# Latents expanded one token tile behind their projection, both roots in one computation, three landing buffers

## The chip, the cores and the metric

The kernel runs on one core of one Trainium2 chip. The time is device microseconds of one execution of the whole program. A core has these engines, each with its own instruction stream, which it works off in order: TensorE (PE) for matrix products and transposes, VectorE (DVE) and ScalarE (ACT) for elementwise work, GpSimd (POOL) for elementwise work too, and SyncE (SP), which issues most loads and stores. ScalarE issues loads as well (those of the feed-forward weights). Engines wait for each other by semaphores.

## The reference

A trunk of two layers over 512 latent tokens and 256 context tokens, width 1024, all in float32. Each layer: a modulated RMS norm, one input projection whose columns are split over four mixers (latent attention, retention, neighbourhood attention, windowed attention), an output projection, a gated residual, then a SwiGLU block. In the last layer the context tokens only give keys and values. The part that the change touches is the latent attention (MLA):

```python
def qkv(cq, ckv, kr, rotate):                     # cq: 256 columns, ckv: 128, kr: 32
    q  = heads(rms_norm(cq,  q_norm)  @ w_uq,  H)  # 256 -> 4 x 96
    kv = heads(rms_norm(ckv, kv_norm) @ w_ukv, H)  # 128 -> 4 x (64 + 64)
    ...
# rms_norm(x, g) = x * rsqrt(mean(x * x) + EPS) * g
```

So each token has two latents, a query and a key/value one; each is normalised by the reciprocal root of its own mean square and expanded by a matrix. Retention, which the kernel computes beside it, goes through chunks of 128 tokens in both directions: scores times a decay mask, plus queries times a state that is updated from chunk to chunk.

## The kernel before

Tokens are worked on in six tiles of 128: 0 to 3 are latent tokens, 4 and 5 context. Layer 0 takes them in the order 4, 5, 0, 1, 2, 3, layer 1 in the order 0 to 5. Every float32 product is computed as three products of rounded halves, high x high, high x low, low x high (L467 to L469), added in PSUM. A weight unit (512 KB as a rule) is loaded into a landing buffer "raw", copied to its high half "wh" by ScalarE (L449), and the rest is put in "wl" by a subtraction (L213), two times in three on VectorE and the third time on GpSimd. There are four landing buffers, five wh and seven wl; a landing buffer is free again when its wl is done.

A program-side list scheduler puts the instructions of each engine in order before anything runs: it goes by readiness and priority, so that code written in one place is spread out and mixed with others. The order that comes out is fixed; a buffer's reuse, a store ahead of it in SyncE's queue, or an instruction ahead of it on its engine can then make an instruction wait.

Around the change a layer goes like this. The retention projection (L1206 to L1228) writes queries, keys and values out and computes chunk states; L1246 updates the running states on VectorE, each a 64 x 64 multiply and add. Then comes the latent stage: `mla_proj` (L961) is a generator that does one token tile per step, and between its steps the caller starts retention chunks (`ret_chunk`, L1250). One step of the generator:

- 24 matmuls of 416 columns (the projection) into PSUM "pg", for which there are five buffers;
- ScalarE copies 384 columns to "cn", in one of two buffers named "nat" (L1052), which retention and the key split use too; two squares with a running sum give the two mean squares (L1056, L1057);
- for each latent, VectorE adds EPS (L1061) and computes the reciprocal root by `rsqrt1` (L287 to L291, eight instructions on one column, results scaled by RS1, which is divided out of w_uq and w_ukv in L966 and L973 by GpSimd);
- TensorE transposes cn (L1067), ScalarE copies the high half "cth" (L1071), VectorE subtracts to the low half "ctl" (L1072);
- six matmuls expand to queries and three to keys and values, "po"; scaled copies with the roots follow (L1080 to L1096), the key part through `k_split` (L686) and transposes (L693).

A retention chunk loads its rows (ldr, L1252), transposes, multiplies by query decays on GpSimd ("rt", L1262), forms scores (L1267), masks them on VectorE ("P", L1270) and multiplies with values (L1282) and states (L1278). At the end `merge_ret` (L1308) loads finished rows into one of two buffers "og". Here is one root as it was:

```python
def rsqrt1(a, nm):
    y = S("rs_y" + nm, 1); u = S("rs_t" + nm, 1)
    ...
    for c in (-3.0, -12.0, -768.0):
        dve.scalar_tensor_tensor(u, y, a, y, op0=ALU.mult, op1=ALU.mult)
        dve.scalar_tensor_tensor(y, u, c, y, op0=ALU.add, op1=ALU.mult)
```

Of the kernel before, what the change touches and what calls it, by code (L numbers as in the profile page):

```python
# [11 lines left out]
ALU = mybir.AluOpType  # L12
# [4 lines left out]
P = 128  # L17
# [6 lines left out]
EPS = 1e-6  # L24
RS1 = -8192.0
# [49 lines left out]

CHANGED = {'pad': {'raw': 1024}, 'bufs': {'raw': 4}}


def merged(opts):
# [6 lines left out]
def build(tc, I, out, opts=None):  # L88
# [36 lines left out]
    def T(tag, shape, dt=F32, bufs=None):  # L125
        uid[0] += 1
        if not PADB:
            return sb.tile(list(shape), dt, tag=tag, name=f"{tag}_{uid[0]}", bufs=bufs or BUFS[tag])
        st = site(tag)
        n = int(np.prod(shape[1:]))  # L130
        x = sb.tile([P, PADB[tag]], dt, tag=st, name=f"{tag}_{uid[0]}", bufs=SPB.get(st, BUFS[tag]))[0:shape[0], 0:n]
        if len(shape) == 2:
            return x
        names = "abcd"[:len(shape) - 1]
        return x.rearrange("p (%s) -> p %s" % (" ".join(names), " ".join(names)), **dict(zip(names, shape[1:])))

    def S(tag, n, bufs=3):
        uid[0] += 1
        return sb.tile([P, n], F32, tag=tag, name=f"{tag}_{uid[0]}", bufs=bufs)
# [104 lines left out]
    def vec(name, k0=0, n=1):  # L244
        i, r = VROW[name]
        return vecs[i][:, r + k0:r + k0 + n]
# [281 lines left out]
    def nat_block(w, c0, n, hT, order, rng=None, filler=None, nf=0, nxt=None):  # L528


        W = ahead.pop(c0, None) or load_nat(w, c0, n)
        for i, t in enumerate(order):
            if nxt and i == PF.get(nxt[0], 9):
                ahead[nxt[0]] = load_nat(w, *nxt)
            a, b = rng(t) if rng else (0, n)
            if a is None:
                continue
            ps = PS("g")
            for k in range(8):
                mm3(ps[:, a:b], hs(hT, t, k), (W[k][0][:, a:b], W[k][1][:, a:b]), k == 0, k == 7)  # L540
                if nf and k % (8 // nf) == 8 // nf - 1:
                    next(filler, None)
            yield t, ps
# [267 lines left out]
    for l in range(LAYERS):  # L811
# [4 lines left out]
        hT = hn  # L816
# [144 lines left out]
        def mla_proj(R):  # L961
# [1 line left out]
            raw = T("raw", [P, 2, 384])  # L963
            sp.dma_start(raw, I["mla_w_uq"][l].rearrange("(k p) n -> p k n", p=P))
            for i in range(2):
                pool.tensor_scalar(raw[:, i], raw[:, i], vec("qn%d" % l, i), 1.0 / RS1, op0=ALU.mult, op1=ALU.mult)  # L966
            wuqh = T(WU, [P, 2, 384], F32R)
            wuql = T(WU, [P, 2, 384], F32R)
            act.activation(wuqh, raw, AF.Copy)
            sub_lo(wuql, raw, wuqh)  # L970
            raw = T("raw", [P, 512])
            sp.dma_start(raw, I["mla_w_ukv"][l])
            pool.tensor_scalar(raw, raw, vec("kn%d" % l), 1.0 / RS1, op0=ALU.mult, op1=ALU.mult)  # L973
            wukv = (T("gate", [P, 512], F32R), T("gate", [P, 512], F32R))
            act.activation(wukv[0], raw, AF.Copy)
            sub_lo(wukv[1], raw, wukv[0])
# [67 lines left out]
                act.activation(d, pt[0:DR, 0:n * P], AF.Copy)  # L1044
                dve.tensor_tensor(d[32:64], pt[32:64, 0:n * P], d[32:64].bitcast(F32), op=ALU.subtract)

            for t, ps in nat_block(w_in, 0, 416, hT, order, (lambda t: (0, 416) if (t < 4 or not last) else (160, 416))):
                qn = t < 4 or not last
                a0 = 0 if qn else 256
                ss = S("ssm", 2)  # L1050
                cn = T("nat", [P, 384])
                act.activation(cn[:, a0:384], ps[:, a0:384], AF.Copy)  # L1052
                KRE.tensor_copy(R[:, t, :], ps[:, 384:416])
                sq = T(SQT, [P, 384])
                if qn:
                    act.activation(sq[:, 0:256], cn[:, 0:256], AF.Square, scale=1.0 / 16.0, accum_out=ss[:, 0:1])  # L1056
                act.activation(sq[:, 256:384], cn[:, 256:384], AF.Square, scale=float(128 ** -0.5), accum_out=ss[:, 1:2])  # L1057
                r = [None, None]
                for c in ((1, 0) if qn else (1,)):
                    ms = S("msm%d" % c, 1)  # L1060
                    dve.tensor_scalar(ms, ss[:, c:c + 1], EPS, None, op0=ALU.add)  # L1061
                    r[c] = rsqrt1(ms, "mk"[c])
                rq, rk = r
                pt = PS(M0)
                k0 = 0 if qn else 2
                for i in range(k0, 3):
# [30 lines left out]
                k_stack(kTm, kn, H, t, M3)  # L1097
                if t in (3, 5):
                    k_rope(t)
                yield mla_attn  # L1100

        def swa_proj():
# [435 lines left out]
```

## Time and profile before

| What | Value |
|---|---|
| Median of 3 runs | 1908.55 us (1906.93 to 1913.02) |
| The profiled execution itself | 1910.68 us |
| Its span, first to last instruction | 1908.8 us |
| TensorE busy | 1811.7 us, 95% |
| VectorE busy | 1187.5 us, 62% |
| ScalarE, GpSimd busy | 672.9 and 605.2 us |
| Mean granted TensorE clock | 0.985 of full speed |

How to read it: the span is that of the profiled execution, some 2 us shorter than what the device measures for it. Busy times of the engines lie beside each other, so they don't add up; an engine's idle time matters only where another one waits for it at the end of a chain. The granted clock of TensorE has two levels, 2.4 GHz (1.00) and 1.2 GHz (0.50); a stretch in between has some of each.

### The profile page before, as it was taken

How to read it: one execution, taken by the hardware profiler on the slowest of the kernel's cores; microseconds unless marked ns; L12 is line 12 of the kernel's file. 1: busy time of each engine (PE TensorE's matmuls, PEld its weight loads, DVE VectorE, ACT ScalarE, POOL GpSimd, SP SyncE). 2: the span in 40 equal slices, each digit the busy share in tenths (PEclk: the TensorE clock that was granted, in tenths of full speed). 3: DMA queues.
4: the chain of work that ended last, by engine and by line, in shares of the span. 5: the costliest groups of instructions: out<-in, count | busy, mean ns of one | idle time of the engine just before them, and what ended most of it. 6: DMA issues, size and time to landing. Idle time of an engine off the chain costs nothing. (4 is left out here: it accounts for less than half of the span.)

```text
span 1908.8 us, 28192 instructions
## 1 busy us (share of the span) xinstructions
PE 1811.7 (95%) x10447; PEld 1494.0 (78%) x10447; DVE 1187.5 (62%) x2676; ACT 672.9 (35%) x1517; POOL 605.2 (32%) x560
## 2 busy tenths in 40 slices
PE   6899999889999999999999999899889999999997
PEld 3677777778889887888888878788777888888885
DVE  5696886877898757564434293465588863434335
ACT  3325643254542221221122233564255532222223
POOL 0211113323115443444344111211333144645542
PEclk9999999899999999999999999999999999999999
DMA  7675436445124346342222222422443033232321
GB/s 226 210 206 162 131 98 187 127 151 117 50 95 127 122 155 199 105 134 63 74 67 67 57 84 91 120 75 81 143 142 100 15 115 101 84 107 89 102 86 44
DMA packets 193555, 215.22 MB, mean 113 GB/s; under 512 B 66660, under 2 KB 141578, under 8 KB 193418
## 3 DMA queue, kind: packets, MB, share of 16 engines
q10 hardware_dynamic: 75840, 111.17, 18.8%
q1 hardware_dynamic: 117578, 102.25, 18.1%
q8 instruction: 82, 1.34, 0.3%
q14 instruction: 55, 0.45, 0.1%
HBM read 192.76 MB, written 20.63 MB: 112 GB/s over the span
## 5 line engine op out<-in xcount | busy, mean ns | idle before, releaser
L469 PE MATMUL pg<-wh,b 128*128 128x512 f32 (+2 forms) x1128 | 439.9, 394 | 7.2 <-POOL b L213 6.2
L467 PE MATMUL pg<-wh,b 128*128 128x512 f32 (+2 forms) x1128 | 443.1, 393 | 1.8 <-ACT b L515 0.9
L468 PE MATMUL pg<-wl,b 128*128 128x512 f32 (+2 forms) x1128 | 441.5, 391 | 2.2 <-DVE rs_yn L288 1.8
L467 PE MATMUL ps<-b,wh 128*128 128x512 f32 (+1 forms) x1120 | 388.2, 347 | 0.0
L469 PE MATMUL ps<-b,wl 128*128 128x512 f32 (+1 forms) x1120 | 386.7, 345 | 0.8 <-DVE wl L213 0.8
L468 PE MATMUL ps<-b,wh 128*128 128x512 f32 (+1 forms) x1120 | 386.9, 345 | 0.5 <-POOL b L213 0.5
L213 DVE TENSOR_TENSOR wl<-raw,wh 128x1024 fp32r<-128x1024 f32 (+1 forms) x131 | 207.4, 1592 | 174.9 <-ACT wh L449 145.3
L449 ACT ACTIVATE wh<-raw 128x1024 fp32r<-128x1024 f32 (+1 forms) x196 | 203.8, 1049 | 271.1 <-PE pg L469 172.3
L213 POOL TENSOR_TENSOR wl<-raw,wh 128x1024 fp32r<-128x1024 f32 (+1 forms) x65 | 160.0, 2462 | 336.7 <-ACT wh L449 286.8
L1362 POOL TENSOR_TENSOR b<-b,nat 128x512 f32<-128x512 f32 (+1 forms) x204 | 217.8, 1087 | 124.0 <-DVE nat L1360 95.0
L469 PEld LDWEIGHTS pg<-wh,b 128*128 128x128 f32 x1128 | 214.9, 191 | 49.6 <-POOL b L213 9.6
L467 PEld LDWEIGHTS pg<-wh,b 128*128 128x128 f32 x1128 | 215.5, 191 | 40.9 <-ACT b L1476 1.9
L468 PEld LDWEIGHTS pg<-wl,b 128*128 128x128 f32 x1128 | 215.2, 191 | 39.7 <-DVE rs_yn L288 2.3
L467 PEld LDWEIGHTS ps<-b,wh 128*128 128x128 f32 x1120 | 213.5, 191 | 27.4 <-issue 2.4
L469 PEld LDWEIGHTS ps<-b,wl 128*128 128x128 f32 x1120 | 213.4, 191 | 26.0 <-DVE wl L213 1.0
L468 PEld LDWEIGHTS ps<-b,wh 128*128 128x128 f32 x1120 | 213.6, 191 | 25.5 <-POOL b L213 0.7
L1360 DVE TENSOR_TENSOR nat<-pg,gate 128x512 f32<-128x512 f32 x240 | 161.9, 688 | 102.0 <-PE pg L469 97.8
L1473 ACT ACTIVATE P<-ps 128x512 f32<-128x512 f32 (+1 forms) x70 | 35.4, 505 | 224.3 <-PE ps L469 128.0
L1475 DVE TENSOR_TENSOR P<-ps,P 128x512 f32<-128x512 f32 (+1 forms) x70 | 40.1, 575 | 118.9 <-PE ps L469 118.8
L1476 ACT ACTIVATE b<-P 128x512 fp32r<-128x512 f32 (+1 forms) x70 | 37.6, 538 | 195.3 <-DVE P L1475 176.0
L397 DVE SCALAR_TENSOR_TENSOR PT<-qT,consts,PT 128x512 f32<-128x512 f32 x112 | 94.0, 857 | 14.6 <-DMA qT<-in_ada_w_dram 13.3
L213 POOL TENSOR_TENSOR b<-P,b 128x512 fp32r<-128x512 f32 (+1 forms) x24 | 27.8, 1158 | 231.9 <-ACT b L1476 231.9
(322 smaller groups left out, 2441.7 us busy)
## 6 DMA issues: line engine op xcount, KB each, us to landing
raw<-in_ffn_w_dram ACTq DMA_DIRECT2D x132, 512.0 KB
qT<-in_ada_w_dram ACTq DMA_DIRECT2D x96, 256.0 KB
raw<-in_w_in_dram SPq DMA_DIRECT2D x40, 512.0 KB
a<-in_ada_w_dram SPq DMA_DIRECT2D x32, 256.0 KB
a<-in_ada_w_dram ACTq DMA_DIRECT2D x32, 256.0 KB
xn<-in_ada_w_dram ACTq DMA_DIRECT2D x32, 256.0 KB
raw<-in_w_out_dram SPq DMA_DIRECT2D x16, 512.0 KB
ldq<-q_d SPq DMA_DIRECT2D x40, 128.0 KB
```

The source lines that it names most:

```text
L213: eng.tensor_tensor(out, full, hi.bitcast(F32), op=ALU.subtract)
L397: dve.scalar_tensor_tensor(acc[s], w, sS[:, k, s:s + 1], acc[s], op0=ALU.mult, op1=ALU.add)
L449: act.activation(hi, raw_ap, AF.Copy)
L467: pe.matmul(ps, a[0], b[0], start=first, stop=False)
L468: pe.matmul(ps, a[0], b[1], start=False, stop=False)
L469: pe.matmul(ps, a[1], b[0], start=False, stop=last)
L1360: dve.tensor_tensor(tm, ps, gates[(0 if t < 4 else 2) + b], op=ALU.mult)
L1362: eng.tensor_tensor(ap, ap, tm[:, a:c], op=ALU.add)
L1473: act.activation(s1[j][:, sl], ps, AF.Silu)
L1475: dve.tensor_tensor(s1[j][:, sl], ps, s1[j][:, sl], op=ALU.mult)
L1476: act.activation(gh[j][:, sl], s1[j][:, sl], AF.Copy)
```

## The change

The number of landing buffers "raw" goes from 4 to 3. One step of the generator is split in two functions: `latent` (copy of cn, mean squares, roots) and `expand` (transposes and all that follows). A tile is expanded after the latents of the next one have been taken; the last is expanded right behind its own. cn lies in an "og" buffer instead of a "nat" one. Both mean squares of a tile go through one `rsqrt` of two columns (one column for the context tiles of layer 1), and the scale RS1 is gone from the two weights.

```diff
--- before.py
+++ after.py
@@ -75,7 +75,7 @@
 
 
 
-CHANGED = {'pad': {'raw': 1024}, 'bufs': {'raw': 4}}
+CHANGED = {'pad': {'raw': 1024}, 'bufs': {'raw': 3}}
 
 
 def merged(opts):
@@ -963,14 +963,14 @@
             raw = T("raw", [P, 2, 384])
             sp.dma_start(raw, I["mla_w_uq"][l].rearrange("(k p) n -> p k n", p=P))
             for i in range(2):
-                pool.tensor_scalar(raw[:, i], raw[:, i], vec("qn%d" % l, i), 1.0 / RS1, op0=ALU.mult, op1=ALU.mult)
+                pool.tensor_scalar(raw[:, i], raw[:, i], vec("qn%d" % l, i), 1.0, op0=ALU.mult, op1=ALU.mult)
             wuqh = T(WU, [P, 2, 384], F32R)
             wuql = T(WU, [P, 2, 384], F32R)
             act.activation(wuqh, raw, AF.Copy)
             sub_lo(wuql, raw, wuqh)
             raw = T("raw", [P, 512])
             sp.dma_start(raw, I["mla_w_ukv"][l])
-            pool.tensor_scalar(raw, raw, vec("kn%d" % l), 1.0 / RS1, op0=ALU.mult, op1=ALU.mult)
+            pool.tensor_scalar(raw, raw, vec("kn%d" % l), 1.0, op0=ALU.mult, op1=ALU.mult)
             wukv = (T("gate", [P, 512], F32R), T("gate", [P, 512], F32R))
             act.activation(wukv[0], raw, AF.Copy)
             sub_lo(wukv[1], raw, wukv[0])
@@ -1044,23 +1044,26 @@
                 act.activation(d, pt[0:DR, 0:n * P], AF.Copy)
                 dve.tensor_tensor(d[32:64], pt[32:64, 0:n * P], d[32:64].bitcast(F32), op=ALU.subtract)
 
-            for t, ps in nat_block(w_in, 0, 416, hT, order, (lambda t: (0, 416) if (t < 4 or not last) else (160, 416))):
+            def latent(t, ps):
+
                 qn = t < 4 or not last
                 a0 = 0 if qn else 256
                 ss = S("ssm", 2)
-                cn = T("nat", [P, 384])
+                cn = T("og", [P, 384])
                 act.activation(cn[:, a0:384], ps[:, a0:384], AF.Copy)
                 KRE.tensor_copy(R[:, t, :], ps[:, 384:416])
                 sq = T(SQT, [P, 384])
                 if qn:
                     act.activation(sq[:, 0:256], cn[:, 0:256], AF.Square, scale=1.0 / 16.0, accum_out=ss[:, 0:1])
                 act.activation(sq[:, 256:384], cn[:, 256:384], AF.Square, scale=float(128 ** -0.5), accum_out=ss[:, 1:2])
-                r = [None, None]
-                for c in ((1, 0) if qn else (1,)):
-                    ms = S("msm%d" % c, 1)
-                    dve.tensor_scalar(ms, ss[:, c:c + 1], EPS, None, op0=ALU.add)
-                    r[c] = rsqrt1(ms, "mk"[c])
-                rq, rk = r
+                n = 2 if qn else 1
+                ms = S("msm", 2)
+                dve.tensor_scalar(ms[:, 0:n], ss[:, 2 - n:2], EPS, None, op0=ALU.add)
+                r = rsqrt(ms[:, 0:n], n, "m%d" % n)
+                return cn, qn, r[:, 0:1], r[:, n - 1:n]
+
+            def expand(t, cn, qn, rq, rk):
+
                 pt = PS(M0)
                 k0 = 0 if qn else 2
                 for i in range(k0, 3):
@@ -1097,6 +1100,14 @@
                 k_stack(kTm, kn, H, t, M3)
                 if t in (3, 5):
                     k_rope(t)
+
+            behind = []
+            for t, ps in nat_block(w_in, 0, 416, hT, order, (lambda t: (0, 416) if (t < 4 or not last) else (160, 416))):
+                behind.append((t,) + latent(t, ps))
+                if len(behind) > 1:
+                    expand(*behind.pop(0))
+                if t == order[-1]:
+                    expand(*behind.pop(0))
                 yield mla_attn
 
         def swa_proj():
```

`rsqrt`, which was there before for retention's eight columns:

```python
def rsqrt(a, n, nm):
    y = S("rs_y" + nm, n); u = S("rs_t" + nm, n)
    dve.tensor_scalar(y.bitcast(I32), a.bitcast(I32), 1, None, op0=ALU.logical_shift_right)
    dve.tensor_scalar(y.bitcast(I32), y.bitcast(I32), -1, 0x5F3759DF, op0=ALU.mult, op1=ALU.add)
    for _ in range(3):
        dve.tensor_tensor(u, y, y, op=ALU.mult)
        dve.scalar_tensor_tensor(u, u, -0.5, a, op0=ALU.mult, op1=ALU.mult)
        dve.scalar_tensor_tensor(y, u, 1.5, y, op0=ALU.add, op1=ALU.mult)
```

Because of the scheduler the change moves instructions in many places. Three of them, in the order of the program; a row has a line, an operation, its output and inputs (tile names with their numbers) and the size. In the kernel after, lines from L1044 on are shifted (L1246 becomes L1257, L1270 becomes L1281, L1067 becomes L1070, L1072 becomes L1075).

SyncE, second w_in block of layer 0, before:

```order
L419 DMA nat_1054<-in_ada_b_dram 2x2x128 x4
L459 DMA raw_1071<-in_w_in_dram 128x2x512
L459 DMA raw_1077<-in_w_in_dram 128x2x512
L424 DMA mod_d_67<-nat_1053 2x2x128 x4
L459 DMA raw_1083<-in_w_in_dram 128x2x512
L898 DMA r_d_122<-nat_1065 128x256
L459 DMA raw_1089<-in_w_in_dram 128x2x512
L904 DMA qn_d_121<-nat_1065 128x256
```

and after:

```order
L419 DMA nat_1054<-in_ada_b_dram 2x2x128 x4
L459 DMA raw_1071<-in_w_in_dram 128x2x512
L459 DMA raw_1077<-in_w_in_dram 128x2x512
L888 DMA v_d_123<-o_890 128x256
L424 DMA mod_d_67<-nat_1053 2x2x128 x4
L459 DMA raw_1083<-in_w_in_dram 128x2x512
L459 DMA raw_1089<-in_w_in_dram 128x2x512
L898 DMA r_d_122<-nat_1065 128x256
```

The fourth w_in load (raw_1089) now stands ahead of the store of nat_1065, not behind it; with three buffers it needs the one of raw_1071.

VectorE, start of layer 0's latent stage, before (b_843 to b_846 hold retention's states, P_3777 is the first chunk's masked score tile, ps_3779 its scores):

```order
L1246 SCALAR_TENSOR_TENSOR b_843_3715<-b_845_3717,gC_3012,b_800_3444 64x64 x4
L1246 SCALAR_TENSOR_TENSOR b_843_3715<-b_843_3715,gC_3012,b_799_3443 64x64 x6
L1222 TENSOR_TENSOR rt_3706<-nat_3699,kd_3006 128x256
L1216 SCALAR_TENSOR_TENSOR nat_3699<-nat_3699,pg_3674 128x256
L1222 TENSOR_TENSOR rt_3706<-nat_3699,kd_3006 128x256
L1246 SCALAR_TENSOR_TENSOR b_843_3715<-b_843_3715,gC_3012,b_799_3443 64x64 x2
L1246 SCALAR_TENSOR_TENSOR b_846_3718<-b_846_3718,gC_3012,b_800_3444 64x64 x4
L1270 TENSOR_TENSOR P_3777<-ps_3779,b_705_2985 128x2x128
L1270 TENSOR_TENSOR P_3778<-ps_3779,b_706_2986 128x2x128
L1270 TENSOR_TENSOR P_3777<-ps_3784,b_705_2985 128x2x128
```

and after:

```order
L1257 SCALAR_TENSOR_TENSOR b_843_3715<-b_845_3717,gC_3012,b_800_3444 64x64 x4
L1257 SCALAR_TENSOR_TENSOR b_843_3715<-b_843_3715,gC_3012,b_799_3443 64x64 x8
L1233 TENSOR_TENSOR rt_3706<-nat_3699,kd_3006 128x256
L1227 SCALAR_TENSOR_TENSOR nat_3699<-nat_3699,pg_3674 128x256
L1233 TENSOR_TENSOR rt_3706<-nat_3699,kd_3006 128x256
L1257 SCALAR_TENSOR_TENSOR b_846_3718<-b_846_3718,gC_3012,b_800_3444 64x64 x2
L1257 SCALAR_TENSOR_TENSOR b_845_3717<-b_843_3715,gC_3012,b_799_3443 64x64 x4
L1257 SCALAR_TENSOR_TENSOR b_846_3718<-b_846_3718,gC_3012,b_800_3444 64x64 x2
L1281 TENSOR_TENSOR P_3777<-ps_3779,b_705_2985 128x2x128
L1281 TENSOR_TENSOR P_3778<-ps_3779,b_706_2986 128x2x128
L1281 TENSOR_TENSOR P_3777<-ps_3784,b_705_2985 128x2x128
```

Ahead of the first P stand 16 updates before and 20 after.

TensorE, the expansion of the last tile but one in layer 0, before (nat_4481 is that tile's cn, po_4519 and po_4535 its expansions, pu the merge of retention, pg_4649 the last tile's projection):

```order
L468 MATMUL pg_4649<-wl_3630,b_90_333 128x416
L1067 MATMUL po_4511<-consts,nat_4481 128x128
L693 MATMUL ps_4446<-consts,nat_4442 128x128 x4
L1067 MATMUL po_4511<-consts,nat_4481 128x128 x2
L469 MATMUL pg_4649<-wh_3629,b_91_334 128x416
L1315 MATMUL pu_4764<-consts,og_4762 128x128 x4
L1315 MATMUL pu_5117<-consts,og_5115 128x128 x4
L467 MATMUL po_4519<-P_4019,cth_4515 128x384
L468 MATMUL po_4519<-P_4020,cth_4515 128x384
L469 MATMUL po_4519<-P_4019,ctl_4516 128x384
L467 MATMUL po_4519<-P_4019,cth_4515 128x384
```

and after (og_4501 is that tile's cn, pg_4563 the last tile's projection, og_4589 the last tile's cn):

```order
L469 MATMUL pg_4563<-wh_3629,b_91_334 128x416
L1070 MATMUL po_4610<-consts,og_4501 128x128 x3
L467 MATMUL po_4618<-P_4019,cth_4614 128x384
L468 MATMUL po_4618<-P_4020,cth_4614 128x384
L469 MATMUL po_4618<-P_4019,ctl_4615 128x384
L467 MATMUL po_4618<-P_4019,cth_4614 128x384
L468 MATMUL po_4618<-P_4020,cth_4614 128x384
L469 MATMUL po_4618<-P_4019,ctl_4615 128x384
L467 MATMUL po_4634<-gate_4026,cth_4614 128x512
L468 MATMUL po_4634<-gate_4027,cth_4614 128x512
L469 MATMUL po_4634<-gate_4026,ctl_4615 128x512
L1326 MATMUL pu_4710<-consts,og_4708 128x128 x4
```

The merge's eight transposes stood between the transposes of cn and their use; now nothing stands there.

VectorE, the same expansion before, and then the one ahead of it after, with the roots around ctl (rs_y and rs_t are a root's tiles, ssm the mean squares):

```order
L213 TENSOR_TENSOR wl_5305<-raw_5302,wh_5304 128x1024
L1061 TENSOR_SCALAR msm_1020_4499<-ssm_4480 128x1
L287 TENSOR_SCALAR rs_ym_4501<-msm_1020_4499 128x1
L288 TENSOR_SCALAR rs_ym_4501<-rs_ym_4501 128x1
L1061 TENSOR_SCALAR msm_1017_4487<-ssm_4480 128x1
L290 SCALAR_TENSOR_TENSOR rs_tm_4502<-rs_ym_4501,msm_1020_4499 128x1
L287 TENSOR_SCALAR rs_yk_4489<-msm_1017_4487 128x1
L291 SCALAR_TENSOR_TENSOR rs_ym_4501<-rs_tm_4502,rs_ym_4501 128x1
L1072 TENSOR_TENSOR ctl_4516<-po_4511,cth_4515 128x384
```

and after (og_4501's mean squares are in ssm_4500, the tile behind that of ctl_4527):

```order
L1054 COPY b_706_2986<-pg_4475 128x32
L1075 TENSOR_TENSOR ctl_4527<-po_4522,cth_4526 128x384
L1061 TENSOR_SCALAR msm_4507<-ssm_4500 128x2
L275 TENSOR_SCALAR rs_ym_1016_4509<-msm_4507 128x2
L276 TENSOR_SCALAR rs_ym_1016_4509<-rs_ym_1016_4509 128x2
L278 TENSOR_TENSOR rs_tm_1017_4510<-rs_ym_1016_4509 128x2
L279 SCALAR_TENSOR_TENSOR rs_tm_1017_4510<-rs_tm_1017_4510,msm_4507 128x2
L280 SCALAR_TENSOR_TENSOR rs_ym_1016_4509<-rs_tm_1017_4510,rs_ym_1016_4509 128x2
```

Before, the tile's own roots stand ahead of its ctl; after, ctl comes first and the roots behind it are the next tile's.

## Rows read from the trace of the kernel before

**Rows 1.** Page: span; then TensorE's busy us, share, instructions.
```profile
span 1908.8 us, 28192 instructions
...
PE 1811.7 (95%) x10447; PEld 1494.0 (78%) x10447; DVE 1187.5 (62%) x2676; ACT 672.9 (35%) x1517; POOL 605.2 (32%) x560
```

**Rows 2.** Windows: length, busy us per engine (PE first), TensorE's granted clock, DMA.
```profile
337.70:354.80 17.10, 12.43 (x54) 11.10 (x54) 12.04 (x37) 1.47 (x3) 1.45 (x3) 0.50 0.26 77
416.20:419.60 3.40, 3.40 (x10) 2.72 (x9) 3.40 (x15) 2.64 (x6) 0.74 (x1) 0.51 0.88 305
```

**Rows 3.** TensorE's waits, 366 to 437 us: total, times, longest.
```profile
PE po L469 <- DVE rs_yk L288: 3.0, 1, 3.0
PE ps L693 <- DVE nat L686: 0.9, 1, 0.9
PE po L469 <- DVE ctl L1072: 0.7, 1, 0.7
```

**Rows 4.** TensorE's waits, 1395 to 1450 us (layer 1).
```profile
PE po L469 <- DVE ctl L1072: 1.4, 1, 1.4
PE ps L693 <- DVE nat L686: 1.0, 1, 1.0
PE po L467 <- ACT cth L1071: 0.6, 1, 0.6
```

**Rows 5.** Timeline, layer 0, 330 to 343 us: start, us, work [idle before].
```profile
330.24 8.31 DVE L1246 SCALAR_TENSOR_TENSOR b<-b,gC,b 64x64 f32<-64x64 f32 x10
...
335.45 2.34 POOL L213 TENSOR_TENSOR wl<-raw,wh 128x1024 fp32r<-128x1024 f32 x1 [0.37 <-ACT wh L449]
...
340.02 1.84 DVE L1246 SCALAR_TENSOR_TENSOR b<-b,gC,b 64x64 f32<-64x64 f32 x6
...
342.37 0.69 PE L1282 MATMUL ps<-ldr,P 128*128 128x64 f32 x2 [6.71 <-DVE P L1270]
```

**Rows 6.** Timeline, layer 0, VectorE's subtraction and TensorE's wait.
```profile
410.31 2.88 DVE L213 TENSOR_TENSOR wl<-raw,wh 128x1024 fp32r<-128x1024 f32 x1
...
415.49 0.44 PE L469 MATMUL po<-P,ctl 128*128 128x384 f32 x1 [2.99 <-DVE rs_yk L288]
```

**Rows 7.** Groups by line: busy us, mean ns, idle before.
```profile
...
L278 DVE TENSOR_TENSOR rs_tr<-rs_yr 128x8 f32<-128x8 f32 x30 | 8.9, 301 | 0.4
L290 DVE SCALAR_TENSOR_TENSOR rs_tm<-rs_ym,msm 128x1 f32<-128x1 f32 x30 | 8.7, 290 | 0.2 <-DVE msm L1061 0.2
```

**Rows 8.** Timeline, layer 1: one expansion with four projection matmuls as filler.
```profile
1403.36 0.49 PE L1067 MATMUL po<-consts,nat 128*128 128x128 f32 x3
1403.61 0.43 PE L467 MATMUL pg<-wh,b 128*128 128x416 f32 x1
1403.88 0.35 PE L468 MATMUL pg<-wl,b 128*128 128x416 f32 x1
1404.07 0.35 PE L469 MATMUL pg<-wh,b 128*128 128x416 f32 x1
...
1404.41 0.56 DVE L1072 TENSOR_TENSOR ctl<-po,cth 128x384 fp32r<-128x384 f32 x1 [0.57 <-ACT cth L1071]
...
1404.44 0.43 PE L467 MATMUL po<-P,cth 128*128 128x384 f32 x1
```

**Rows 9.** Timeline: GpSimd's scaling of w_uq.
```profile
295.59 1.78 POOL L966 TENSOR_SCALAR raw<-raw,consts 128x384 f32<-128x384 f32 x2 [3.13 <-DMA raw<-in_mla_w_uq_dram]
```

**Rows 10.** Timeline, layer 0, the second w_in block's units.
```profile
119.48 1.47 SPq L459 DMA_DIRECT2D raw<-in_w_in_dram  x2
...
124.53 1.06 ACT L449 ACTIVATE wh<-raw 128x1024 fp32r<-128x1024 f32 x1 [0.96 <-DMA raw<-in_w_in_dram]
...
125.67 2.60 POOL L213 TENSOR_TENSOR wl<-raw,wh 128x1024 fp32r<-128x1024 f32 x1 [33.73 <-ACT wh L449]
...
126.53 0.38 SPq L459 DMA_DIRECT2D raw<-in_w_in_dram  x1
...
136.37 0.50 PE L468 MATMUL pg<-wl,b 128*128 128x512 f32 x1 [0.31 <-POOL wl L213]
```

## The prediction

> **What bounds the kernel now.** I read the page's engine line first: TensorE is busy for 1811.7 of 1908.8 us [rows 1], so it can win back at most the 97 us in which it sits idle, plus what it loses at the lower of its two clocks. The windows come next, to see where in the program such time lies. In the stretch from 337.7 to 354.8 us TensorE runs at a granted clock of 0.50 (1.2 GHz) and is busy for 12.43 us, about 6.2 us more than the same matmuls would take at 2.4 GHz; at 416.2 to 419.6 the clock is 0.51 with 3.40 us of work, so 1.7 us are lost [rows 2]. Both lie in layer 0's latent stage, which the change rewrites. Third, the list of TensorE's waits in this stage of each layer, to see which of them hang on the latents' chain: 3.0, 0.9 and 0.7 us in layer 0 [rows 3], 1.4, 1.0 and 0.6 us in layer 1 [rows 4]. Together 7.6 us. Last, the timeline of the two places where most is at stake [rows 5, 6].
>
> The largest wait of the stage is none of these. TensorE waits 6.71 us for the first masked score tile P of retention (L1270) [rows 5], and the half clock sets in during that wait. VectorE works in order, and P stands there behind 16 state updates (L1246). The first ten take 8.31 us, 0.83 us each, while GpSimd works beside it (a subtraction at 335.45, and others); the next six take 1.84 us, 0.31 each [rows 5].
>
> **The two roots in one, and the expansion one tile later.** Counting by the code, a tile that needs both roots issued 2 x (1 + 2 + 6) = 18 small VectorE instructions and now issues 1 + 2 + 9 = 12; over both layers 198 become 144. At 0.29 us each (0.30 for the 128x8 form, so two columns should cost about the same) [rows 7] that is up to 16 us of VectorE time. TensorE does not wait for VectorE's total, though, only at the places named in the waits, so I give the 54 instructions nothing by themselves. Bounds: 0 and -7.6 us, the sum of those waits.
>
> What the order changes is where the root stands. Before, a tile's root chain surrounds its own ctl (L1072), the low half that the third product of the expansion needs. At 415.49 TensorE waits 2.99 us there; VectorE had just spent 2.88 us on one weight subtraction (L213), and the roots came behind that [rows 6]. After, ctl stands ahead of the next tile's root. The second effect counts against the change: what TensorE has to do between the transposes of the latent and their first use. With four projection matmuls between them the use follows 1.08 us after the transposes begin, with no wait, and ctl ends at 1404.97, 0.53 us after that first use [rows 8]. A projection matmul issues every 0.19 us [rows 8]. An expansion without any filler therefore costs 1.08 - 0.25 = 0.83 us, and one without filler ahead of ctl 0.2 us more (0.53 less two matmuls at about that spacing). In the new order of TensorE the last but one expansion of layer 0 has no filler at either place: 1.0 us. The last has four small transposes: 0.4 us. The other four have 4 or 5 matmuls and are covered. Before, eight transposes of the retention merge and a stretch of the output projection stood at these places; they now come later.
>
> Layer 0: waits of 3.0 + 0.9 + 0.7 = 4.6 go, 1.4 come, and I leave 0.2 for the key transposes (L693), since their multiply still needs the product itself: -3.0 us. With the 3.0 us wait gone I also drop the 1.7 us at half clock behind it. Layer 1: of 1.4 + 1.0 + 0.6 = 3.0 us, 0.5 us remain at the key transposes, 0.5 at the context tiles and 0.5 for fillers missing ahead of ctl: -1.5 us. Bounds over both layers: -9.3 (everything goes, with the clock) and +2 (the two bare expansions and the later merge cost their price, the waits stay).
>
> **The start of the latent stage.** In the new order twenty state updates stand ahead of the first P, not sixteen, and ten projection matmuls, not six, stand ahead of TensorE's first L1282. Four updates cost 1.2 us at the quiet rate and 3.3 us at the rate beside GpSimd; four matmuls give back 0.8 us. GpSimd's scaling of w_uq (L966), which ran early and took 1.78 us for its pair [rows 9], now stands ahead of the product that retention needs (L1262), since its load gets a landing buffer only when the second w_in unit has been split. L973 moves behind that product. That is 0.4 to 2.5 us for the updates, up to 1.8 us more if VectorE is held up throughout L966, and down to -12.9 us (6.71 + 6.2) if the new interleaving happens to close the gap. I take +1 us, near the quiet row: VectorE's new extra updates come when GpSimd waits for later loads.
>
> The Trainium skill (GPSIMD Engine Reference, section 8, "Key points") says that GpSimd shares its SBUF interfaces with VectorE and contends with VectorE instructions of two SBUF inputs, which the state updates are. The trace agrees as far as it goes, 0.83 against 0.31 us; by the rule the end at +4.3 us would be the more likely one.
>
> **Three landing buffers instead of four.** In the FFN the loads are far ahead and TensorE's waits there are not for them: 0. Where loads are late is the second w_in block at 119 us. Its first load is issued at 119.48 and its copy starts at 124.53, 5.05 us later; the fourth load is issued at 126.53 [rows 10]. Now the fourth needs the first one's buffer, which GpSimd's subtraction frees at 125.67 + 2.60 = 128.27. It goes out 1.7 us later and stands ahead of two stores on SyncE. TensorE already waits 0.31 us for that unit's low half [rows 10], so nothing covers the shift: 0 to +1.8 us. I take +1, since TensorE's next wait in that stretch, for the modulation work on VectorE, absorbs some of it.
>
> The Trainium skill (DMA: Bandwidth & Descriptors, section "Anatomy of one DMA") fits a transfer at 2.0 us plus bytes over 436 GB/s, for GpSimd-issued ones; for 512 KB that gives an estimate of 3.2 us. The row has 5.05 us, in a stretch where other loads share the engines. By the page's price the fourth load would land at 131.5 and the term would be near 0; the row decides.
>
> **The sum.** -3.0 - 1.7 - 1.5 + 1 + 1 = -4.2 us. The profiled execution took 1910.68 us, so it would take 1906.5; it is 2.1 us above the median of the runs shown, 1908.55, and against that the forecast is 1904.3 us.
>
> **Rivals.**
> *The gap at 337 us closes.* Ten matmuls of cover and another interleaving with GpSimd bring P in time. Then 6.71 + 6.2 us go and the +1 with them: -5.2 - 12.9 = -18 us, 1890 us. For it: the wait is the largest of the stage and depends on a few GpSimd instructions meeting VectorE. Against it: P now stands behind more updates.
> *The waits only change place.* TensorE's order before already started two or three projections ahead of the first expansion, so the second half of the change's name buys little, and the filler it uses up in one place is missing in another (the bare expansions; the merge and w_out loads that SyncE now issues after the last latents). Gains and prices cancel: 1908 us.
> *Slower: the start of the stage gets longer.* Price: four updates at 0.83 (3.3) and L966 (1.8), less 0.8, make the first wait 4.3 us longer. The second chunk's later P pair now stands behind twelve updates, 3.7 us at the quiet rate and 10.0 at the other, 6.9 if half of them meet GpSimd. One more stretch like that at 416.2 us at half clock is 1.7 us, the late w_in unit 1.8. 4.3 + 6.9 + 1.7 + 1.8 - 6.2 = +8.5: 1917 us. It decides from the point where all twenty updates average 0.8 us or more. For it: GpSimd's work is denser there than before. Against it: later loads may thin it out.
>
> **How the numbers follow.** A measurement of this kernel tells 0.3%, or 5.7 us, from no change. Forecast 0.46, with its own range from 1897 to 1908: half of that lies below 1902.8. Gap closes 0.17; waits change place 0.15; slower 0.22. Faster: 0.24 + 0.17 = 0.41; same: 0.22 + 0.15 = 0.37; slower 0.22. The range goes from 1889, where the closed gap lies, to 1917, the slower rival.
>
> **What would show it.** In the profile after: no wait of TensorE above 1 us on rs_yk or its successor, and no half clock near 416 us; one wait of about 1 us ahead of the last but one expansion's first product; the wait for P between 6 and 9 us with the half clock behind it; the fourth w_in load near 128.3 us and a wait of 1 to 2 us for its low half; the FFN's windows unchanged. The forecast is wrong if the wait for P moves by more than 4 us either way, or if FFN windows lose time for landing buffers.

## The result, and the profile after

The kernel after is slower: 1925.85 us median (1921.55 to 1932.23) against 1908.38 (1905.02 to 1913.02) for the one before on the same chip, a ratio of 1.0096 with a 95% interval of 1.0081 to 1.0112. That is 17.5 us where a gain of 4 was forecast, and above the range's upper end of 1917. The profiled execution of the kernel after took 1921.94 us; the engine line of its page, to be held against [rows 1]:

```profile
span 1920.2 us, 28134 instructions
...
PE 1811.5 (94%) x10447; PEld 1491.9 (78%) x10447; DVE 1189.1 (62%) x2622; ACT 675.2 (35%) x1517; POOL 603.1 (31%) x560
```

TensorE's work is the same (1811.7 to 1811.5 us), so between these two executions the whole difference of 11.4 us of span is idle time, 97.1 to 108.7 us. That is less than the 17.5 us of the medians, because the profiled execution of the kernel before lies 2.3 us above its median and that of the kernel after 3.9 us below its own. VectorE lost the 54 instructions that were counted (2676 to 2622) and none of its busy time. The other executions of the kernel after spread with the granted clock, from 1921.55 us at a mean of 0.985 to 1932.23 at 0.980.

TensorE's waits, summed over stretches of the program (the same bounds in both, so a stretch is off by the drift of a few us):

| Stretch, us | Before | After | Difference |
|---|---|---|---|
| 0 to 150, start and first blocks | 20.4 | 20.0 | -0.4 |
| 150 to 440, layer 0's mixers | 20.9 | 28.0 | +7.1 |
| 440 to 600, layer 0, output projection | 4.0 | 5.8 | +1.8 |
| 600 to 1100, mostly FFN | 9.2 | 6.8 | -2.4 |
| 1100 to 1450, layer 1's mixers | 20.1 | 27.5 | +7.4 |
| 1450 to 1930 | 7.7 | 6.0 | -1.7 |

Together that is +11.8 us, close to the 11.6 us by which idle time grew. The two mixer stages lose, the FFN doesn't. Windows show the same; columns as in [rows 2]. Before:

```profile
332.00:412.00 80.00, 69.72 (x430) 61.44 (x429) 59.23 (x218) 29.50 (x78) 26.84 (x31) 0.89 0.38 118
...
150.00:440.00 290.00, 268.38 (x1763) 216.42 (x1762) 222.08 (x678) 139.17 (x393) 64.85 (x71) 0.96 0.49 146
...
600.00:1100.00 500.00, 490.73 (x2700) 418.92 (x2699) 264.42 (x334) 100.52 (x142) 211.69 (x197) 1.00 0.34 107
```

and after:

```profile
332.00:412.00 80.00, 68.75 (x418) 60.42 (x415) 59.58 (x215) 28.24 (x80) 27.03 (x34) 0.89 0.38 119
...
150.00:440.00 290.00, 262.37 (x1729) 212.12 (x1730) 220.43 (x641) 137.88 (x391) 59.15 (x69) 0.96 0.48 145
...
387.00:394.00 7.00, 6.82 (x43) 6.40 (x44) 3.35 (x13) 1.08 (x5) 1.77 (x2) 0.76 0.13 47
...
424.00:431.00 7.00, 5.28 (x22) 4.66 (x21) 6.49 (x17) 5.52 (x16) 1.88 (x3) 0.76 0.58 192
...
600.00:1100.00 500.00, 493.22 (x2727) 422.09 (x2726) 270.40 (x340) 101.66 (x144) 212.19 (x196) 1.00 0.35 107
```

From 332 to 412 us TensorE gets 418 matmuls done and not 430. The stretch at half clock near 416 [rows 2] is gone, but two others have come, each 7 us at a mean of 0.76, by estimate 1.7 us lost in each. Over 332 to 412 us, where the half clock at the start of the stage falls, the mean is 0.89 in both, and over all of layer 0's mixers 0.96 in both. So here the two executions differ in waits, not in the clock. The FFN runs as before.

The waits behind the latents, layer 0, answer to [rows 3] (TensorE, 374 to 447 us):

```profile
PE ps L693 <- DVE nat L686: 3.4, 2, 1.7
PE pu L1326 <- DMA og<-o_d: 1.8, 1, 1.8
PE po L1042 <- POOL nat L1039: 1.2, 1, 1.2
PE pt L586 <- DVE P L620: 0.6, 1, 0.6
PE po L467 <- ACT cth L1074: 0.6, 1, 0.6
PE pg L467 <- DVE nat L1371: 0.6, 1, 0.6
```

The 3.0 us for a root are gone, as forecast. TensorE now waits at the key transposes (L693), for the merge's load (L1326) and for the rotated keys (L1042) instead; all its waits from 372 to 440 us come to 8.1 us in place of 5.2. The last but one expansion waits 0.6 us (L1074), where about 1 us was forecast. Layer 1, 1404 to 1462 us, against [rows 4]:

```profile
PE po L1042 <- POOL nat L1039: 3.7, 2, 3.1
PE ps L693 <- DVE nat L686: 1.8, 1, 1.8
PE po L469 <- DVE ctl L1075: 1.0, 1, 1.0
PE ps L693 <- DVE rs_ym L280: 0.4, 1, 0.4
```

Here too more is waited for, and elsewhere. The start of layer 0's latent stage, after, against [rows 5] (the DVE L1257 rows are the state updates, L1293 uses the first P; start, us, work [idle before]):

```profile
332.14 7.03 DVE L1257 SCALAR_TENSOR_TENSOR b<-b,gC,b 64x64 f32<-64x64 f32 x12
...
339.54 0.41 DVE L1227 SCALAR_TENSOR_TENSOR nat<-nat,pg 128x256 f32<-128x256 f32 x1
...
340.01 0.46 PE L467 MATMUL pg<-wh,b 128*128 128x416 f32 x1 [3.62 <-DVE nat L1227]
...
340.21 5.33 DVE L1257 SCALAR_TENSOR_TENSOR b<-b,gC,b 64x64 f32<-64x64 f32 x8
...
345.57 1.42 DVE L1281 TENSOR_TENSOR P<-ps,b 128x256 f32<-128x256 f32 x4
...
346.05 0.43 PE L1293 MATMUL ps<-ldr,P 128*128 128x64 f32 x2 [2.62 <-DVE P L1281]
```

One wait of 6.71 us has become two of 3.62 + 2.62 = 6.24. The ten projection matmuls meant as cover need a PSUM buffer that VectorE's L1227 gives back, and L1227 itself stands behind twelve updates. The twenty updates take 12.36 us, 0.62 each, between the two rates of [rows 5]. But 0.62, 0.83 and 0.31 are averages of two kinds of update. Over the whole execution after, and for one update beside one GpSimd subtraction (minimum, median and maximum in ns, and where it starts):

```profile
L1257 DVE SCALAR_TENSOR_TENSOR b<-b,gC,b x64: 269/284/2408, 332.1 to 1381.0; 64x64 f32<-64x64 f32 x64
...
L1257 DVE SCALAR_TENSOR_TENSOR b<-b,gC,b x1: 2408/2408/2408, 340.8 to 340.8; 64x64 f32<-64x64 f32 x1
...
340.80 2.36 POOL L213 TENSOR_TENSOR wl<-raw,wh 128x1024 fp32r<-128x1024 f32 x1 [1.71 <-ACT wh L449]
```

In both traces the median update takes 0.28 us, and one that meets a whole subtraction on GpSimd lasts about as long as that does: 2.41 us beside 2.36 here, and in the kernel before 2.36 us beside the 2.34 of [rows 5]. So what an update costs goes with what it meets, and the number of updates tells little.

The second w_in block against [rows 10], timeline and then TensorE's waits from 124 to 142 us:

```profile
119.82 0.91 SPq L459 DMA_DIRECT2D raw<-in_w_in_dram  x2
...
124.11 1.06 ACT L449 ACTIVATE wh<-raw 128x1024 fp32r<-128x1024 f32 x1 [1.24 <-DMA raw<-in_w_in_dram]
...
125.98 2.67 SPq L459 DMA_DIRECT2D raw<-in_w_in_dram  x2
```

```profile
PE pg L468 <- POOL wl L213: 1.2, 1, 1.2
```

The third and fourth loads form one group that ends at 128.65, so the fourth went out near 128.3 as forecast, and the wait for the low half is 1.2 us, as forecast. At that place the reading was right; the landing buffer cost more elsewhere, as the experiments show.

### The profile page after: what moved, and what is told of

Its sections match the earlier page's. It is cut to its first block, busy times and chain, and to the rows that moved or that the text cites. A ratio compares the mean times of both kernels' runs of the same rounds, so it can differ in the third digit from the quotient of the medians.

```text
span 1920.2 us, 28134 instructions
## 1 busy us (share of the span) xinstructions
PE 1811.5 (94%) x10447; PEld 1491.9 (78%) x10447; DVE 1189.1 (62%) x2622; ACT 675.2 (35%) x1517; POOL 603.1 (31%) x560
## 4 chain that ended last, share of the span: by engine, by line
PE 57%; DVE 11%; DMA 3%; POOL 3%; ACT 2%; issue 2%; SPq 0%; ACTq 0%; DVEq 0%; POOLq 0%
PE ps L467 9%; PE ps L468 9%; PE ps L469 9%; PE pg L469 7%; PE pg L467 7%; PE pg L468 7%; PE ps L633 2%; PE po L599 2%; PE pt L586 2%; DVE wl L213 1%; DVE PT L397 1%; POOL wl L213 1%; ACT wh L449 1%; DMA qT<-in_ada_w_dram 1%; DVE P L620 1%
## 5 line engine op out<-in xcount | busy, mean ns | idle before, releaser
L1486 DVE TENSOR_TENSOR P<-ps,P 128x512 f32<-128x512 f32 (+1 forms) x70 | 40.2, 575 | 110.4 <-PE ps L469 110.2
L213 POOL TENSOR_TENSOR b<-P,b 128x512 fp32r<-128x512 f32 (+1 forms) x24 | 28.1, 1170 | 224.8 <-ACT b L1487 204.9
```

Source lines behind the costliest of these rows:

```text
L213: eng.tensor_tensor(out, full, hi.bitcast(F32), op=ALU.subtract)
L1486: dve.tensor_tensor(s1[j][:, sl], ps, s1[j][:, sl], op=ALU.mult)
```

## The experiments

Three theories stood at first. A: the missing landing buffer carries the loss. B: the expansion one tile behind carries it. C: the order before is a favourable one, and any newly planned order costs some us. Each ratio is against runs of the kernel before on the same chip (medians 1908.2 to 1909.4). "Idle" is the profiled span less TensorE's busy time; "clock" is the mean granted clock of that one execution.

| Kernel | Landing buffers | Median, us | Ratio to before (95%) | Idle, us | Clock |
|---|---|---|---|---|---|
| before | 4 | 1908.38 | 1 | 97.1 | 0.985 |
| e7_swap | 4 | 1918.75 | 1.0057 (1.0042 to 1.0071) | 100.8 | 0.981 |
| e8_before_sq | 4 | 1915.16 | 1.0028 (1.0017 to 1.0039) | 101.0 | 0.986 |
| e3_one_root | 4 | 1916.09 | 1.0048 (1.0029 to 1.0066) | 102.4 | 0.986 |
| e15_rt_raw4 | 4 | 1918.10 | 1.0042 (1.0029 to 1.0055) | 101.6 | 0.986 |
| e2_only_raw3 | 3 | 1917.83 | 1.0051 (1.0034 to 1.0068) | 105.5 | 0.986 |
| e9_raw3_sq | 3 | 1927.89 | 1.0100 (1.0086 to 1.0113) | 107.4 | 0.983 |
| e5_one_root_raw3 | 3 | 1924.99 | 1.0082 (1.0068 to 1.0096) | 106.2 | 0.979 |
| e16_rt_raw3 | 3 | 1923.74 | 1.0078 (1.0062 to 1.0095) | 105.2 | 0.983 |
| after | 3 | 1925.85 | 1.0096 (1.0081 to 1.0112) | 108.7 | 0.985 |
| e6_behind_raw3 | 3 | 1923.43 | 1.0083 (1.0066 to 1.0100) | 107.8 | 0.986 |
| e10_after_sq | 3 | 1926.86 | 1.0091 (1.0075 to 1.0107) | 108.3 | 0.981 |
| e11_after_og3 | 3 | 1925.79 | 1.0082 (1.0066 to 1.0098) | 109.8 | 0.981 |
| e13_after_tail | 3 | 1930.60 | 1.0115 (1.0094 to 1.0136) | 109.5 | 0.985 |
| e18_raw3_wl8 | 3 | 1919.36 | 1.0054 (1.0038 to 1.0070) | 103.1 | 0.983 |
| e20_after_wl8 | 3 | 1928.30 | 1.0104 (1.0088 to 1.0120) | 110.4 | 0.982 |
| e17_sq_raw4 | 4 | 1927.93 | 1.0107 (1.0088 to 1.0127) | 120.7 | 0.985 |
| e19_sq_raw3 | 3 | 1935.92 | 1.0148 (1.0127 to 1.0168) | 124.2 | 0.982 |

Leaving aside the last two, whose loads go through another queue, the idle column sorts the kernels by itself: 97.1 us in the order before, 100.8 to 102.4 in the other orders with four landing buffers, 103.1 to 110.4 with three.

**The landing buffers alone, and the merged root alone.** e2 is the kernel before with three landing buffers; e3 is the kernel before with both roots in one `rsqrt`.

```diff
-CHANGED = {'pad': {'raw': 1024}, 'bufs': {'raw': 4}}
+CHANGED = {'pad': {'raw': 1024}, 'bufs': {'raw': 3}}
```

> The kernel before with three landing buffers instead of four and nothing else. Theory A (the landing buffers carry the loss of 17.5 us: loads wait longer at the head of SyncE's queue and hold up stores and loads behind them): 1920 us or more, with the added waits of TensorE in layer 0 between 280 and 420 us. Theory B (the expansion one tile behind carries it): within 4 us of before, 1905 to 1912. Theory C (any new order costs a few us, since the order before is a favourable one): 1911 to 1918.

> The kernel before with both roots of a tile in one computation of two columns (and the scale RS1 gone), four landing buffers, the expansion right behind its own latents. Theory A and theory B: 1903 to 1910, since neither part that they blame is there and the root is shorter. Theory C (any new order costs a few us): 1911 to 1918.

e2 loses 9.4 us and e3, which saves 54 VectorE instructions, loses 7.7. e2 lies at the upper end of what theory C allows and below what A asked for; e3 fits C alone. Since e3 only saves instructions, its loss can't be their cost, so theory C needed a control.

**The expansion behind, with the two roots as before.** e6 is the kernel after with `rsqrt1` twice, and three landing buffers.

```diff
-                r = rsqrt(ms[:, 0:n], n, "m%d" % n)
...
+                    r[c] = rsqrt1(ms, "mk"[c])
```

> The changed kernel with the two separate roots of before: expansion one tile behind, three landing buffers. If the merged root does nothing for the time, it is within 4 us of the changed kernel, 1922 to 1930. If the merged root is what costs (more VectorE instructions in one chain of eleven, nine of them dependent), it is back near 1908. By theory B it stays near 1926, by theory C it may lie anywhere from 1911 to 1928.

It stands as the kernel after does, 1923.43 us beside 1925.85, within the intervals: the merged root brings nothing beside the other two parts.

**Harmless edits as controls.** e7 writes the two roots of a tile in the other order; e8 exchanges the two squares; nothing else differs from the kernel before. e10 exchanges the squares of the kernel after.

```diff
-                for c in ((1, 0) if qn else (1,)):
+                for c in ((0, 1) if qn else (1,)):
```

> A control: the kernel before with the two roots of a tile written in the other order (query first), nothing added or removed, so that only the planned order of the instructions moves. Theories A and B: 1906 to 1911, as before. Theory C (the order before is a favourable one among many): 3 to 10 us slower, 1911 to 1918.

> A second control: the kernel before with the two squares of a tile written in the other order (key latent first), nothing added or removed. Theory C (the order before is a favourable one, a neighbouring order costs about 8 us): 1913 to 1920. If the first control was an accident: 1906 to 1911.

> The same harmless exchange of the two squares in the changed kernel. If the changed kernel is itself an unlucky order of its kind and its parts cost nothing beyond a lost favourable order, it falls to 1914 to 1920, where the controls and the single parts lie. If the expansion one tile behind with three landing buffers costs some 7 us by itself, it stays at 1921 to 1930.

The same work in another order costs 0.57 and 0.28%, some 10 and 6 us (e7 is just above theory C's range), so theory C holds in its first half: the order before is better than its neighbours. e10 stays at the kernel after's time, so this one exchange gives no sign that the kernel after is an unlucky order.

**Two places of the stage's end.** e11 gives the kernel after a third og buffer; e13 expands the last three tiles of a layer right behind their own latents (the last one was already expanded so; the expectation says two).

```diff
+CHANGED = {'pad': {'raw': 1024}, 'bufs': {'raw': 3, 'og': 3}}
...
-                if t == order[-1]:
+                if t in order[-3:]:
```

> The changed kernel with three og buffers instead of two, so that retention's merge no longer waits for the last latents to leave theirs. If the late merge is what the expansion one tile behind costs (in the changed kernel TensorE waits 1.8 us for og<-o_d behind the last expansions, and the merge no longer fills their gaps), 4 to 8 us faster than the changed kernel: 1918 to 1922, with that wait gone. If not: 1923 to 1929.

> The changed kernel with the last two tiles of a layer expanded right behind their own latents, the others one tile behind. If the bare expansions at the end of the stage cost what was forecast for them (1.4 us in layer 0), 1 to 3 us faster than the changed kernel, 1923 to 1925; by the theory that only the neighbourhood of the order counts, anywhere from 1914 to 1928.

Neither gives anything back. But e11 didn't do what it was meant to: TensorE still waits 1.9 us for og<-o_d (1.8 in the kernel after), so it says nothing of what the late merge costs. In e13 that wait is gone, and the time is 1930.60, above every range that was set. It moved waits too: those for a latent's high half (cth) went from 0.6 to 1.8 us and those for the rotated keys (L1042) in layer 0 from 1.2 to 3.6. In e16 below both waits are gone, og<-o_d and cth, and it stands at 1.0078 beside the kernel after's 1.0096, within the intervals. So the late merge and the bare expansions, though the waits show them, carry a small part of the 17.5 us at most, by these runs.

**Pairs with four and with three landing buffers, all else alike in the code.** e15 and e16 are the whole change but with cn in an "rt" buffer (for cn in "og" there is no room beside four landing buffers); e5 is e3, and e9 is e8, with three.

```diff
-                cn = T("og", [P, 384])
+                cn = T("rt", [P, 384])
```

> The changed kernel (one root, expansion one tile behind) with four landing buffers; so that it fits in memory, cn lies in one of the three rt buffers instead of an og buffer. If the landing buffers carry the part of the loss that goes beyond the controls (they lie at 1915 and 1919), 1915 to 1920, with the wait for ldq<-qn_d in layer 1 back at 3 us. If the expansion one tile behind carries it: 1922 to 1929.

> The same kernel (cn in rt) with three landing buffers, as the partner of the run with four. If the landing buffers cost something under this change too: 5 to 10 us above its partner, with the wait for ldq<-qn_d in layer 1 above 5 us. If not: within 4 us of it.

> The kernel before with both roots in one computation and three landing buffers, expansion right behind its own latents: the whole change without the shift by one tile. If the shift costs 6 to 9 us, as the difference between the changed kernel and three buffers alone suggests: 1914 to 1920. If the three parts only add up in any combination: 1922 to 1928.

> The kernel before with three landing buffers and the two squares exchanged (a harmless exchange of order), as a second sample of three buffers alone. If three buffers cost about 2.5 us in layer 1 (a wait for ldq<-qn_d) and the rest of their 9.4 us is the lost order: 1915 to 1921. If three buffers cost more than any exchange of order: 1922 or more.

From four to three: e15 to e16 +5.6 us, e3 to e5 +8.9, e8 to e9 +12.7. The last two pairs were measured on different chips; by the ratios, which take each chip's own runs of the kernel before, the three are 6.9, 6.5 and 13.7 us. Theory B has two runs against it. e15, with expansion behind, one root and four landing buffers, stands at 1.0042, in the middle of the controls' 1.0028 to 1.0057. And e5, the whole change without the shift, stands at 1924.99 us beside the kernel after's 1925.85. So the shift and the merged root neither gain nor lose a measurable amount against another newly planned order, as far as these few orders show. In one point e15 missed: its wait for ldq<-qn_d was 5.6 us and not back at 3. The pages of e8 and then of e9:

```profile
span 1911.4 us, 28184 instructions
...
PE 1810.4 (95%) x10447; PEld 1491.3 (78%) x10447; DVE 1192.6 (62%) x2676; ACT 672.4 (35%) x1517; POOL 608.3 (32%) x560
```

```profile
span 1927.5 us, 28212 instructions
...
PE 1820.1 (94%) x10447; PEld 1497.2 (78%) x10447; DVE 1201.4 (62%) x2676; ACT 674.5 (35%) x1517; POOL 603.1 (31%) x560
```

Idle time grows by 6.4 us and the busy time of the same matmuls by 9.7, at a mean clock of 0.983 in place of 0.986. In the other two of these pairs idle grows by 3.8 and 3.6 us and busy by 8.2 and 8.3. How much of that is the kernels' own can't be read from one execution each: those of e8, e3 and e15 ran at 0.986, above the mean of their kernels' executions (0.9845, 0.9840 and 0.9838). Over all executions the mean clock falls by 0.0025 from e8 to e9 and by 0.0024 from e3 to e5, but only from 0.9838 to 0.9835 from e15 to e16, which still loses 5.6 us. So a lower clock is no regular part of what the landing buffer costs.

**By which way the landing buffer costs.** Theory Q: a weight load that waits for a buffer stands at the head of SyncE's queue and holds up the mixers' stores and loads behind it. Theory D: weights are staged less far ahead, whatever the queue. e17 and e19 have the mixers' weight loads on ScalarE, with four and with three buffers; e18 and e20 give the freed memory to an eighth wl. The edits (of long lines only the part that differs):

```diff
-... 'so': 'sp', 'sp_': 'sp'} ...
+... 'so': 'sp', 'sp_': 'sp', 'wn': 'act'} ...
...
-... 'bufs': {'raw': 3}}
+... 'bufs': {'raw': 3, 'wl': 8}}
```

> The kernel before with its four landing buffers, but with the weight loads of the mixers (L459) issued by ScalarE and not by SyncE. It is the base of a pair with e19. A new order costs some 8 us by the runs so far, so both theories expect 1912 to 1925 us here; what counts is the distance to e19.

> The same with three landing buffers. Theory Q: with three buffers a weight load waits for its buffer at the head of SyncE's queue and holds up the mixers' stores and loads behind it; with the loads on ScalarE that is gone, and e19 is at most 4 us above e17. Theory D: the weights are split less far ahead whatever queue issues their loads; e19 is 7 us or more above e17, like the four pairs so far (5.6 to 12.7).

> The kernel before with three landing buffers and the memory of the fourth given to an eighth buffer wl. Theory D with depth counted over both kinds of buffers: a subtraction finds its wl free earlier and hands back the landing buffer earlier, so half or more of e2's loss goes against a re-planned order: 1910 to 1915 us. If only the landing buffers count, as theory Q needs: as e2, 1916 to 1921 us.

> The kernel after with an eighth buffer wl. Theory D over both kinds of buffers: 1914 to 1921 us. If only the landing buffers count: as the kernel after, 1922 to 1929 us.

e17 lies 2.9 us above the upper end of its range and above every other order with four landing buffers; why isn't shown. The difference stays, +8.0 us, like the other pairs, which speaks against Q; but the two intervals just touch (1.0127 ends one and begins the other), so it isn't excluded that some of it went. Nor did the waiting of loads end; a part of it moved to ScalarE. In e19 ScalarE stands idle twice behind one of these loads until a subtraction frees a landing buffer, in e17 nowhere (ScalarE's timeline; ACTq issues the load):

```profile
53.39 0.44 ACTq L459 DMA_DIRECT2D raw<-in_w_in_dram  x1
54.18 0.38 ACT L329 ACTIVATE rt<-po 128x256 f32<-128x256 f32 x1 [3.26 <-POOL wl L213]
...
345.44 0.39 ACTq L459 DMA_DIRECT2D raw<-in_w_out_dram  x1
345.87 0.38 ACT L1213 ACTIVATE nat<-pg 128x256 f32<-128x256 f32 x1 [2.25 <-POOL wl L213]
```

The eighth wl gives nothing back (1919.4 beside e2's 1917.8, 1928.3 beside the kernel after's 1925.9). It moves the order too, so this speaks against staging depth over both kinds of buffers without excluding it. One wait grows in every pair, that for the neighbourhood queries' loads in layer 1 (L669). TensorE's waits from 1170 to 1260 us, e17 and then e19:

```profile
PE pu L693 <- DVE nat L683: 4.6, 1, 4.6
PE pt L669 <- DMA ldq<-qn_d: 4.1, 1, 4.1
```

```profile
PE pt L669 <- DMA ldq<-qn_d: 8.9, 1, 8.9
PE pu L693 <- DVE nat L683: 0.5, 1, 0.5
```

But the wait ahead of it shrinks by nearly as much, 8.7 to 9.4 us together. So this shows that the place exists, not that it carries the 8 us.

## Why the prediction was wrong, point by point

*The landing buffers* are the step that failed most clearly. The prediction costed them at "+1", with an upper end of 1.8, from the one block where it saw loads late. There it was right (1.2 us of wait). But the four pairs of newly planned orders give +5.6, +8.9, +12.7 and +8.0 us, a mean of 8.8 (8.7 by the ratios), more than the 5.5 us between the controls (1.0028 to 1.0057). The error was to take one place for the whole: from the kernel before to the kernel after the waits of 150 to 440 and 1100 to 1450 us grew by 7 us each without any single one above 6 us.

*The sum stood on an unstated premise*, that the rest of the order stays what it is. The four other orders that keep four landing buffers and SyncE's queue lie at 1.0044 on average, 8 us above the kernel before, two of them after an exchange of two lines. This term was missing, and no row of the kernel before shows it. 8 + 9 = 17 us, against the 17.5 measured, but this close a sum is partly luck. The two don't add up strictly: e2, a new order too, loses only 9.4 with three buffers, so either its order kept what was good in the old one, or the buffer costs less there.

*The latents' waits in layer 0 (-3.0) and the half clock behind them (-1.7).* The 3.0 us wait did go and so did the stretch near 416. But the waits of 372 to 440 us grew by 2.9 us, and half clock came at 387 and 424. What the prediction held for a rival, "the waits only change place", is what these terms did. It also misread what made the 3.0 us. The 2.88 us subtraction of [rows 6] met a subtraction on GpSimd, while one that meets none takes 1.22 us (before, then after):

```profile
409.74 2.37 POOL L213 TENSOR_TENSOR wl<-raw,wh 128x1024 fp32r<-128x1024 f32 x1
...
423.68 1.22 DVE L213 TENSOR_TENSOR wl<-raw,wh 128x1024 fp32r<-128x1024 f32 x1 [1.25 <-ACT wh L449]
```

So by estimate more than half of that wait, 2.88 - 1.22 = 1.66 us, came from a meeting of the two engines and not from where the root stands. In layer 1 the waits change place too: -1.5 us was forecast for the latents' waits, and all waits between 1360 and 1450 us grew by 4.5 (11.0 to 15.5).

*The start of the stage (+1).* The stretch from 330 to 372 us waits for 8.6 and not 7.8 us: +0.8. That the term came out near +1 is luck, for it came by a way that wasn't foreseen. The wait for P fell by 4.1 us, more than the 4 us named as the sign of a wrong forecast, but 3.62 us for L1227 took its place, since the cover itself hung on VectorE. The slower rival (a longer first wait, from 0.8 us per update) is not what happened: the updates averaged 0.62. The term and that rival both priced an update at 0.31 or 0.83 us each, which is no price of one update: the median is 0.28 us, and one that meets a subtraction on GpSimd takes that one's time. The Trainium skill (GPSIMD Engine Reference, section 8, "Key points") has GpSimd contend with VectorE instructions of two SBUF inputs. The trace agrees, with 2.41 us beside a subtraction of 2.36 and a median of 0.28.

*The merged root (0)* and *the FFN (0)* were right: e6 and the kernel after agree, and the FFN's waits went from 9.2 to 6.8 us. The 0.29 us per small instruction, which the sum doesn't use, is the mean of 30 of which one took 1.51; the median is 0.21.

**What stays open.** Which waits carry the landing buffer's 9 us could not be pinned down: waits grow in many small places, idle time by only 3.5 to 6.4 us in the four pairs, and what makes up the rest isn't shown. Going from four to three buffers also makes the scheduler write another order, so that buffer and order can't be told apart within a pair, only over several. Nor is it shown what makes the order before better than its neighbours; its idle time is 97.1 us where theirs is 101 to 102. That VectorE meets GpSimd at other places in each order is a candidate, and no run tests it. No version tried beats the kernel before.

## What to carry to other kernels

Where a scheduler re-plans the whole program, measure first what a harmless exchange costs: if that alone is 0.3 to 0.6%, a gain of 0.2% summed up from single waits is below it, and the sum of waits says little. Price a buffer that is taken away over every stage where it is used, not at the one place where a load is seen to be late. And a wait taken off TensorE is a gain only where the engine that is next late has been named: here it was VectorE again in most places (L1227, L1281, L686).

## What the runs showed that was not expected

Exchanging two independent squares moved 1909 us to 1915. The mean of some small VectorE instructions moved without their being changed: L278 on eight columns took 301 ns before [rows 7] and takes 211 ns after. The median did not move (before, then after; minimum, median and maximum in ns):

```profile
L278 DVE TENSOR_TENSOR rs_tr<-rs_yr x30: 152/166/1529, 358.6 to 1400.6; 128x8 f32<-128x8 f32 x30
...
L278 DVE TENSOR_TENSOR rs_tr<-rs_yr x30: 147/166/674, 359.3 to 1410.9; 128x8 f32<-128x8 f32 x30
```

The one of 1529 ns starts at 1389.8 us and ends with a GpSimd subtraction that runs from 1389.52 for 1.83 us. So a few meetings with GpSimd make the mean, and a new order deals them out anew. VectorE's total, 1187.5 to 1189.1 us, shows nothing of the 54 instructions that were saved. A list of means by line hides this; minimum, median and maximum show it.
